# High parts of two weights fetched anew by GpSimd instead of kept, in a single-core decoder layer, with the planner's numbers and the order of stages set anew

## The chip, the cores and the metric

The kernel runs on one core of one Trainium2 chip. The metric is the device time of one execution in microseconds. Three runs of the kernel before took 2396.77, 2397.39 and 2397.78 us; the median, 2397.39, is what the changed kernel is compared with. A separate execution was profiled; its span, from the first to the last instruction, is 2396.1 us.

## What is computed

One layer on 2048 tokens of width 1024, in float32. The reference, cut to its core:

```python
h = rms_norm(x, mix_norm_g)
z = h @ w_in                                   # 1024 x 2048
lru_x, lru_gate, conf_a, conf_b = split(z, 4)  # 512 columns each
y_lru = rg_lru(causal_dwconv(lru_x), ...) * gelu(lru_gate)
c = silu(layer_norm(causal_dwconv(conf_a * sigmoid(conf_b))))   # 31 taps
x = x + concatenate([y_lru, c]) @ w_out        # 1024 x 1024
q = rms_norm(x) @ w_q;  k, v = split(rms_norm(mem) @ w_kv, 2)   # 256 memory tokens
x = x + softmax(q k / 16) v @ w_o              # 4 heads of 256
g, u = split(rms_norm(x) @ w_up, 2)            # 1024 x 6144
x = x + (gelu(causal_dwconv(g)) * u) @ w_down  # 3072 x 1024
return rms_norm(x)
```

## The kernel before, in words

**Products in three passes.** A float32 operand is split into a high half, rounded to the type float32r by a ScalarE (ACT) copy, and a low half, which VectorE (DVE) makes by subtracting the high half from the operand (`split`, line 578). `mm3` (line 586) then multiplies high by high, high by low and low by high. The tiles are called wh and wl for a weight, Xh/Xl, xh/xl, yh/yl and hidh/hidl for activations. Nearly all of TensorE's work is such triples of 128x512 matmuls.

**Tiles and quarters.** The sequence is cut into four quarters of 512 tokens. A *mixer* per quarter (`mixer`, with `conf` and `lru`) multiplies by `w_in`, in 8 groups of 256 columns, and runs the convolutions and the recurrence. For each group and each half kq of the rows, `project` (line 700) asks for two pairs (wh, wl) of 128 rows by 4 blocks by 128 columns, 256 KB a tile. Quarters 0 and 1 then go through attention one by one (`attend`, line 1254), and quarters 2 and 3 together (`attend_pair`, line 1760), in a form that needs fewer products and reads combined weights from `Folds`. Then come the up projection (`up` and `strassen_cols`) for each half of the sequence, and the down projection (`Down`). The memory's keys and values are folded into two matrices A and VO early on (`memory_a`, `memory_vo`), among the mixers.

**Where the weights come from.** A class for each of the two layouts hands them out:

- `Columns` (line 647) serves `w_in`. On the first call for a group it loads the raw columns (512 KB in pieces of 1 KB), splits them and, since they are wanted four times, writes all four tiles to a scratch area in DRAM (`Kept`, line 608) as rows of 2 KB. On later calls (n > 1) it reads both halves back from there.
- `Rows` (line 679) does the same for `w_out`, by 128 rows and 512 columns. With no raw weight (w is None) it hands out A and VO, which exist only in the scratch area.

All these transfers are issued by SyncE (SP), each after the semaphores that it needs: a store after its split, a load after the store of the same tile and after the last reader of the buffer that it goes into. GpSimd (POOL) issues only some small setup transfers at the start and computes nothing but the identity matrix.

**What sets the order.** Every operation and transfer is first recorded (`Program.do`, `Program.dma`, which is why the profile shows one line, L399, the emitter, for all of them). Generators for the stages are stepped by `drive`, in the order of the list TURNS and by a clock that counts TensorE work; each `yield n` gives way for n us of that clock. This fixes TensorE's order and which buffers follow each other. Then `deadlines` (line 239) gives every operation a due time, backwards from the products, and `schedule` (line 260) plays the program through: each engine takes the ready operation that is due first, 84 tiles of 2 KB a partition (slots "S") are handed out in order, and a transfer takes bytes / DMA_RATE on its issuer's own lane plus DMA_DELAY. Three passes are made, and the one that ends first is emitted. So DMA_DELAY, DMA_RATE and HOP_SAME (the assumed delay between two instructions of one engine) decide in which order each engine's queue is written, not what is in it.

**The constants around line 1976** are the waits and paces of the stages: for instance MEM_WAIT (when the memory's stage begins), MIX_WAIT and MIX_PACE (how the mixers are spread), EARLY (how many of the up projection's seven operand sets are made before it begins), FOLD_PACE and PAIR_WAIT (the pair's weights and its normalisations), NORMED (when each quarter's layer norm is done), and TURNS.

Of the kernel before, what the change touches and what calls it, by code (L numbers as in the profile page):

```python
# [17 lines left out]
P = 128  # L18
# [3 lines left out]
KQ = NK // 2  # L22
TT = 512
NQ = S // TT
# [24 lines left out]


HOP = 0.3
HOP_SAME = 0.1
DMA_DELAY = 2.5
DMA_RATE = 300e3
ACT_SWITCH = 1.3
ACT_PATIENCE = 8.0
POOL_LAST = 6.0
ISSUE = dict(SP=0.1, ACT=0.3, Pool=1.0)
# [74 lines left out]
class Program:  # L133
# [68 lines left out]
        o.calls.append((name, (out,) + args, kw))  # L202
        self.touch(o, [r.buf for r in ins] + list(reads), [r.buf for r in outs] + list(writes))

    def dma(self, out, in_, reads=(), writes=(), join=False, slack=30, by="SP"):


        o = self.op(by)
        o.moves = True
        refs = [r for r in (out, in_) if isinstance(r, Ref)]  # L210
        nbytes = max(int(np.prod(r.dummy.shape)) for r in refs) * 4
        o.cost, o.delay = nbytes / DMA_RATE, DMA_DELAY
        o.calls.append(("dma_start", (), dict(out=out, in_=in_)))
        rd = [in_.buf] if isinstance(in_, Ref) else []
        wr = [out.buf] if isinstance(out, Ref) else []
        o.store = slack if rd else False
        self.touch(o, rd + list(reads), wr + list(writes), join)
# [42 lines left out]
    def schedule(self):  # L260
# [3 lines left out]
        idle = {e: True for e in self.engines}  # L264
        free = {t: list(range(n)) for t, n in SLOTS.items()}
        queues = {t: list(reversed(q)) for t, q in self.queues.items()}
        table, dma_free, lag = [None], {e: 0.0 for e in ISSUE}, [0.0]
        order = []

        def push(t, kind, x):  # L270
            seq[0] += 1
            heapq.heappush(events, (t, seq[0], kind, x))
# [49 lines left out]
        def dispatch(e, t):  # L322
            if not idle[e]:
                return
            o = pick(e, t)
            if o is None:
                return
            idle[e] = False
            o.start, o.on = t, e
            order.append(o)  # L330
            if e == "PE":
                lag[0] += 0.2 * (t - o.turn - lag[0])
            cost = o.cost
            if e == "ACT" and o.sets is not None and table[0] not in o.sets:
                cost += ACT_SWITCH
                table[0] = o.sets[0]
            if o.either and e == "DVE":
                cost = estimate("DVE", "tensor_tensor", 1024, False)
            if o.moves:
                dma_free[e] = max(dma_free[e], t) + cost  # L340
                push(t + ISSUE[e], 2, e)
                push(dma_free[e] + o.delay, 0, o)
            else:
                push(t + cost, 2, e)
                push(t + cost, 0, o)
# [12 lines left out]
        while events:  # L358
            t, _, kind, o = heapq.heappop(events)
# [10 lines left out]
            else:  # L370
                for s in o.succs:
                    satisfied(s, t + (HOP_SAME if s.eng == o.on else HOP))
                for b in o.bufs:
# [49 lines left out]
def hybrid_layer(  # L423
# [17 lines left out]
    pr = Program(nc, place)  # L441
# [29 lines left out]
    def rnd(name, shape=None):  # L471
        return pr.new("S", shape, F32R, name)
# [7 lines left out]
    def spawn(gen, before=None):  # L480
        t = Task(gen)
        tasks.insert(tasks.index(before) if before else len(tasks), t)
        return t
# [160 lines left out]
    def flat(b):  # L644
        return Ref(b, (lambda ap: ap.rearrange("p k f -> p (k f)"),), np.broadcast_to(np.int8(0), (P, TT)))

    class Columns:
# [6 lines left out]
        def get(self, c0, kq):  # L654
            key = (c0, kq)
            n = self.seen[key] = self.seen.get(key, 0) + 1
            base = ((c0 // (2 * P)) * 2 + kq) * 4
            if n > 1:
                return [tuple(self.kept.get(base + 2 * f + i, (P, KQ, P), "w" + "hl"[i]) for i in range(2)) for f in range(2)]
            st = self.early.pop(key, None) or raw_cols(self.w, c0, kq)  # L660
            got = self.rounded(c0, kq, st)
            if n < self.uses:
                self.store(c0, kq, got)
            return got
# [5 lines left out]
        def rounded(self, c0, kq, st):  # L670
            return [split_cols(st, f) for f in range(2)]

        def store(self, c0, kq, got):
            base = ((c0 // (2 * P)) * 2 + kq) * 4
            for f in range(2):
                for i in range(2):
                    self.kept.put(base + 2 * f + i, flat(got[f][i]))

    class Rows:

# [4 lines left out]
        def get(self, k, half):  # L685
            base = (k * 2 + half) * 2
            n = self.seen[k, half] = self.seen.get((k, half), 0) + 1
            if n > 1 or self.w is None:
                return tuple(self.kept.get(base + i, None, "w" + "hl"[i]) for i in range(2))
            st = tmp("raw")  # L690
            pr.dma(st[:], self.w[k * P : (k + 1) * P, half * TT : (half + 1) * TT])
            hi, lo = pair("w")
            split(st[:], hi, lo)
            if n < self.uses:
                self.kept.put(base, hi[:])
                self.kept.put(base + 1, lo[:])
            return hi, lo

# [380 lines left out]
    attended = [Task(None) for _ in range(NQ)]  # L1079
# [893 lines left out]
        yield V_LATE  # L1973
        vec["v3072"] = columns([ffn_conv_w[0], ffn_conv_b], DFF, "v3072")

    EARLY, VO_WAIT, V_LATE, Z_COPIED = 5, 2, 500, (0, 1)
    MIX_WAIT, MIX_TURN, LN_SUM, LN_SQ, GATES = (5, 7, 6, 0), 5, 6, 0, 3
    MIX_PACE, ATT_PACE = (1, 4, 3, 4), ((0, 3, 0), (0, 2, 2), (6, 3, 3), (5, 9, 0))
    PAUSE, WARM = 2, 16
    FED = ("B21", "T2", "T1", "T3")  # L1980
    MEM_WAIT, VO_LATE, ATT_TURN, FFN_TURN, X_PACE, T_PACE = 17, 10, 1, (3, 8, 7, 24), 3, 10

    FOLDED = (2, 3)
    PAIR_WAIT, PAIR_TURN, FOLD_PACE = (0, 0, 9, 17), 7, (6, 7, 35)
    EARLY_AT, KEPT_AT = 6, 5
    FOLD_AT = lambda: ([turned_x[0]], [mem_a, turned_x[1]], [mem_vo])
    F_out, F_a, F_vo = Folds(W_out, "t_out"), Folds(A_rows, "t_a"), Folds(VO_rows, "t_vo")

    NORMED = [lambda: ([m[0]], 108), lambda: ([attended[0]], 31), lambda: ([m[2]], 26), lambda: ([m[3], n[2]], 6)]
    ATTEND = [lambda: [n[0]], lambda: [n[1]]]  # L1990
    TURNS = lambda: [later, first, fold, m[0], mem_a, m[1], first_t, a[0], n[2], m[3], n[0], n[3], mem_vo, n[1], m[2], a[1], a[2], tail]
    X = [HalfX(h) for h in range(NH)]

    def first_x():
# [6 lines left out]
    def feed_forward():  # L2001
        yield first
        yield attended[NQ - 1]
        spawn(X[1].kept(attends[NQ - 1], 20), tail)
        spawn(prepare_down(), tail)
        yield from up(0, X[0], X[1].make)
        down = Down()

        def ahead(key):
            if key in FED:  # L2010
                down.feed(0, FED.index(key))

        yield from up(1, X[1], ahead)
        yield from down.run()

    mixers, normeds, attends = ([Task(None) for _ in range(NQ)] for _ in range(3))
    later, mem_a, mem_vo, first_t, first, tail = (Task(None) for _ in range(6))
    m, n, a = mixers, normeds, attends
    for q in range(NQ):
        m[q].gen = mixer(q, m[q - 1] if q else None)  # L2020
        n[q].gen = normed(q, *NORMED[q]())
        if q not in FOLDED:
# [3 lines left out]
    fold = Task(fold_weights())  # L2026
# [36 lines left out]
```

## Time and profile before

| | |
|---|---|
| median of 3 runs | 2397.39 us (2396.77 to 2397.78) |
| span of the profiled execution, the only time given for it | 2396.1 us |
| TensorE (PE) busy | 2382.6 us, 99% |
| VectorE (DVE) busy | 2034.0 us, 85% |
| ScalarE (ACT) busy | 1313.2 us, 55% |
| GpSimd (POOL) busy | 11.2 us |
| HBM read, written | 409.36 MB, 192.94 MB |

How to read it: matmuls are pipelined, and the records give each a modelled end, so two that follow each other at full rate overlap and "busy" is the union of them. PEld is the loading of the weights into TensorE, which overlaps the products. A row of the waits gives the engine and what it writes, what ended the wait, the total in us, the number of waits and the longest. A row of a group gives its count, then busy time and mean ns of one, then the idle time of the engine just before it. A row of a transfer gives its issuer with a small q, the number of issues, the KB of each and the median us from issue to landing.

### The profile page before, as it was taken

The page shows a single profiled execution, that of the slowest core. Times are in us where ns is not written, and L with a number is a line of the kernel's source. Part 1 is how long each engine was busy: PE and PEld are TensorE (multiplying, and loading weights), DVE is VectorE, ACT ScalarE, POOL GpSimd, SP SyncE. Part 2 cuts the span into 40 slices and gives each one's busy share as a digit, 9 for nine tenths or more (in the row PEclk, how much of TensorE's full clock was granted, in tenths as well). Part 3 has the DMA queues.
Part 4 walks back from the last instruction along what each step waited for, and adds up shares of the span by engine and source line. Part 5 has one row for each costly group of instructions (what it writes and reads, how often), then busy time and mean ns, then how long its engine had stood idle before and what let it go on. Part 6 is the DMA issues. An engine that isn't in the chain of part 4 may idle for free.

```text
span 2396.1 us, 33483 instructions
## 1 busy us (share of the span) xinstructions
PE 2382.6 (99%) x10948; PEld 1974.5 (82%) x10948; DVE 2034.0 (85%) x3355; ACT 1313.2 (55%) x2374; POOL 11.2 (0%) x26
## 2 busy tenths in 40 slices
PE   9999999999999999999999999999999999999998
PEld 7898888888887888888888888888888888888887
DVE  7999994299899869879999887988988896676787
ACT  7772776357557678695555555554555541222333
POOL 1000000000000000000000000000000000000000
PEclk9999999999999999999999999999999999999999
DMA  9598789775878988787766544556565589887986
GB/s 351 197 296 309 234 300 305 254 255 176 296 261 271 318 277 280 268 289 265 252 234 208 194 172 158 175 177 211 190 216 199 186 303 324 283 280 254 312 303 258
DMA packets 363912, 604.56 MB, mean 252 GB/s; under 512 B 34809, under 2 KB 116985, under 8 KB 363738
## 3 DMA queue, kind: packets, MB, share of 16 engines
q1 hardware_dynamic: 362952, 601.81, 73.8%
q8 instruction: 86, 1.41, 0.2%
q14 instruction: 88, 0.72, 0.1%
q0 software_dynamic: 640, 0.36, 0.0%
q10 hardware_dynamic: 146, 0.27, 0.0%
HBM read 409.36 MB, written 192.94 MB: 251 GB/s over the span
## 4 chain that ended last, share of the span: by engine, by line
PE 94%; DVE 2%; ACT 2%; DMA 1%; issue 1%; SPq 0%; POOL 0%; DVEq 0%; POOLq 0%; ACTq 0%
PE ps L399 94%; DMA wl<-w_down 1%; DVE conv L399 1%; ACT L399 0%; DMA raw<-in_w_kv_dram 0%; ACT wh L399 0%; DVE wl L399 0%; ACT gate L399 0%; DVE x L399 0%; DVE s L399 0%; ACT yh L399 0%; DVE smalls L399 0%; DVE ptl L399 0%; ACT prob L399 0%; ACT conv L399 0%
## 5 line engine op out<-in xcount | busy, mean ns | idle before, releaser
L399 PE MATMUL ps<-Xh,wh 128*128 128x512 f32 x1344 | 523.3, 389 | 0.7 <-ACT u L399 0.7
L399 PE MATMUL ps<-Xh,wl 128*128 128x512 f32 x1344 | 523.2, 389 | 0.7 <-DVE wl L399 0.5
L399 PE MATMUL ps<-Xl,wh 128*128 128x512 f32 x1344 | 523.0, 389 | 0.0
L399 PE MATMUL ps<-wh,hidh 128*128 128x512 f32 x960 | 374.4, 390 | 0.0
L399 PE MATMUL ps<-wh,hidl 128*128 128x512 f32 x960 | 374.2, 390 | 0.1
L399 PE MATMUL ps<-wl,hidh 128*128 128x512 f32 x960 | 373.7, 389 | 0.0
L399 DVE SCALAR_TENSOR_TENSOR conv<-cb,v,conv 128x512 f32<-128x512 f32 x480 | 334.9, 741 | 1.8 <-ACT conv L399 0.9
L399 PEld LDWEIGHTS ps<-Xh,wl 128*128 128x128 f32 x1344 | 252.3, 188 | 54.0 <-DVE wl L399 1.5
L399 PEld LDWEIGHTS ps<-Xh,wh 128*128 128x128 f32 x1344 | 252.3, 188 | 53.1 <-ACT u L399 1.1
L399 PEld LDWEIGHTS ps<-Xl,wh 128*128 128x128 f32 x1344 | 252.3, 188 | 52.5
L399 ACT ACTIVATE hidh<-s 128x512 fp32r<-128x512 f32 x186 | 113.8, 631 | 271.6 <-DVE s L399 227.9
L399 PEld LDWEIGHTS ps<-wh,hidl 128*128 128x128 f32 x960 | 180.2, 188 | 39.5 <-DVE hidl L399 2.1
L399 PEld LDWEIGHTS ps<-wh,hidh 128*128 128x128 f32 x960 | 180.2, 188 | 37.8 <-ACT hidh L399 0.4
L399 PEld LDWEIGHTS ps<-wl,hidh 128*128 128x128 f32 x960 | 180.3, 188 | 37.2 <-DMA wl<-w_down 0.4
L399 PE MATMUL ps<-xh,wh 128*128 128x512 f32 x512 | 204.0, 398 | 0.1
L399 PE MATMUL ps<-xl,wh 128*128 128x512 f32 x512 | 199.6, 390 | 0.3 <-DVE xl L399 0.3
L399 PE MATMUL ps<-xh,wl 128*128 128x512 f32 x512 | 199.6, 390 | 0.0
L399 ACT ACTIVATE wh<-s 128x512 fp32r<-128x512 f32 x192 | 119.6, 629 | 117.6 <-DVE s L399 79.1
L399 ACT ACTIVATE wh<-raw 128x512 fp32r<-128x512 f32 (+2 forms) x214 | 127.4, 613 | 53.1 <-PE ps L399 21.6
L399 ACT ACTIVATE u<-ps 128x512 f32<-128x512 f32 x144 | 85.7, 595 | 126.0 <-PE ps L399 125.2
L399 DVE TENSOR_TENSOR acc<-acc,ps 128x512 f32<-128x512 f32 (+1 forms) x157 | 102.7, 678 | 59.5 <-PE ps L399 56.4
L399 DVE TENSOR_TENSOR wl<-raw,wh 128x512 fp32r<-128x512 f32 (+2 forms) x214 | 140.2, 668 | 12.0 <-ACT wh L399 10.7
(256 smaller groups left out, 4014.2 us busy)
## 6 DMA issues: line engine op xcount, KB each, us to landing
raw<-in_w_up_dram SPq DMA_DIRECT2D x96, 512.0 KB, 4.5
wh<-w_down SPq DMA_DIRECT2D x156, 256.0 KB, 4.9
wl<-w_down SPq DMA_DIRECT2D x156, 256.0 KB, 5.0
w_down<-wh SPq DMA_DIRECT2D x144, 256.0 KB, 3.1
w_down<-wl SPq DMA_DIRECT2D x144, 256.0 KB, 3.5
h<-hid SPq DMA_DIRECT2D x120, 256.0 KB, 4.7
wh<-w_in SPq DMA_DIRECT2D x96, 256.0 KB, 4.2
wl<-w_in SPq DMA_DIRECT2D x96, 256.0 KB, 4.7
```

The costliest lines, as they stand in the source:

```text
L399: getattr(e, name)(*[resolve(a) for a in args], **{k: resolve(a) for k, a in kw.items()})
```

## The change

Three things change.

1. `Columns.store` writes the low tiles alone, and `Rows.get` too. On later calls for `w_in` and `w_out` the high tile is made by a transfer from the raw float32 weight into a float32r tile, issued by GpSimd, and the low tile is read back as before. For `w_in` such a transfer reads 128 rows by 4 blocks in pieces of 512 bytes; for `w_out` 128 rows of 2 KB. A and VO stay as they were.
2. The planner's numbers: HOP_SAME, DMA_DELAY, DMA_RATE, and one lane that all issuers share instead of one for each.
3. The constants of the stages and the list TURNS.

```diff
-HOP_SAME = 0.1
-DMA_DELAY = 2.5
-DMA_RATE = 300e3
+HOP_SAME = 0.05
+DMA_DELAY = 5
+DMA_RATE = 350e3
...
-        table, dma_free, lag = [None], {e: 0.0 for e in ISSUE}, [0.0]
+        table, dma_free, lag = [None], [0.0], [0.0]
...
-                dma_free[e] = max(dma_free[e], t) + cost
+                dma_free[0] = max(dma_free[0], t) + cost
                 push(t + ISSUE[e], 2, e)
-                push(dma_free[e] + o.delay, 0, o)
+                push(dma_free[0] + o.delay, 0, o)
...
             if n > 1:
-                return [tuple(self.kept.get(base + 2 * f + i, (P, KQ, P), "w" + "hl"[i]) for i in range(2)) for f in range(2)]
+                return [self.again(c0 + f * P, kq, base + 2 * f + 1) for f in range(2)]
...
+        def again(self, c0, kq, low):
+            hi = rnd("wh", (P, KQ, P))
+            pr.dma(hi[:], self.w[kq * KQ * P : (kq + 1) * KQ * P, c0 : c0 + P].rearrange("(k p) f -> p k f", p=P), by="Pool")
+            return hi, self.kept.get(low, (P, KQ, P), "wl")
+
         def store(self, c0, kq, got):
             base = ((c0 // (2 * P)) * 2 + kq) * 4
             for f in range(2):
-                for i in range(2):
-                    self.kept.put(base + 2 * f + i, flat(got[f][i]))
+                self.kept.put(base + 2 * f + 1, flat(got[f][1]))
...
-            if n > 1 or self.w is None:
+            if n > 1 and self.w is not None:
+                hi = rnd("wh")
+                pr.dma(hi[:], self.w[k * P : (k + 1) * P, half * TT : (half + 1) * TT], by="Pool")
+                return hi, self.kept.get(base + 1, None, "wl")
+            if self.w is None:
                 return tuple(self.kept.get(base + i, None, "w" + "hl"[i]) for i in range(2))
...
             if n < self.uses:
-                self.kept.put(base, hi[:])
                 self.kept.put(base + 1, lo[:])
...
-    EARLY, VO_WAIT, V_LATE, Z_COPIED = 5, 2, 500, (0, 1)
-    MIX_WAIT, MIX_TURN, LN_SUM, LN_SQ, GATES = (5, 7, 6, 0), 5, 6, 0, 3
-    MIX_PACE, ATT_PACE = (1, 4, 3, 4), ((0, 3, 0), (0, 2, 2), (6, 3, 3), (5, 9, 0))
-    PAUSE, WARM = 2, 16
+    EARLY, VO_WAIT, V_LATE, Z_COPIED = 2, 3, 500, (0, 1)
+    MIX_WAIT, MIX_TURN, LN_SUM, LN_SQ, GATES = (5, 8, 10, 0), 4, 7, 0, 3
+    MIX_PACE, ATT_PACE = (0, 4, 3, 4), ((0, 3, 2), (0, 2, 0), (0, 0, 0), (0, 0, 0))
+    PAUSE, WARM = 1, 16
     FED = ("B21", "T2", "T1", "T3")
-    MEM_WAIT, VO_LATE, ATT_TURN, FFN_TURN, X_PACE, T_PACE = 17, 10, 1, (3, 8, 7, 24), 3, 10
+    MEM_WAIT, VO_LATE, ATT_TURN, FFN_TURN, X_PACE, T_PACE = 20, 11, 4, (5, 10, 0, 0), 0, 8
...
-    PAIR_WAIT, PAIR_TURN, FOLD_PACE = (0, 0, 9, 17), 7, (6, 7, 35)
+    PAIR_WAIT, PAIR_TURN, FOLD_PACE = (0, 0, 9, 28), 8, (3, 7, 33)
...
-    NORMED = [lambda: ([m[0]], 108), lambda: ([attended[0]], 31), lambda: ([m[2]], 26), lambda: ([m[3], n[2]], 6)]
+    NORMED = [lambda: ([m[0]], 108), lambda: ([attended[0]], 35), lambda: ([m[2]], 43), lambda: ([m[3], n[2]], 18)]
...
-    TURNS = lambda: [later, first, fold, m[0], mem_a, m[1], first_t, a[0], n[2], m[3], n[0], n[3], mem_vo, n[1], m[2], a[1], a[2], tail]
+    TURNS = lambda: [first, later, fold, m[0], mem_a, m[1], a[0], n[2], n[1], n[0], first_t, n[3], mem_vo, m[3], m[2], a[1], a[2], tail]
...
-        spawn(X[1].kept(attends[NQ - 1], 20), tail)
+        spawn(X[1].kept(attends[NQ - 1], 22), tail)
```

More of the change, by code (lines that the diff above doesn't have):

```diff
@@ L203, in do, with dma @@
         self.touch(o, [r.buf for r in ins] + list(reads), [r.buf for r in outs] + list(writes))
-    def dma(self, out, in_, reads=(), writes=(), join=False, slack=30, by="SP"):
+    def dma(self, out, in_, reads=(), writes=(), join=False, slack=30, by="SP", **more):
         o = self.op(by)
@@ L212, in dma @@
         o.cost, o.delay = nbytes / DMA_RATE, DMA_DELAY
-        o.calls.append(("dma_start", (), dict(out=out, in_=in_)))
+        o.calls.append(("dma_start", (), dict(out=out, in_=in_, **more)))
         rd = [in_.buf] if isinstance(in_, Ref) else []
```

## The prediction

> **What bounds the kernel now.** I read the page's head first, then PE's own waits, then a table of PE by stretches, because a kernel whose TensorE is nearly always busy can only win what TensorE still loses.
>
> ```profile
> span 2396.1 us, 33483 instructions
> PE 2382.6 (99%) x10948; PEld 1974.5 (82%) x10948; DVE 2034.0 (85%) x3355; ACT 1313.2 (55%) x2374; POOL 11.2 (0%) x26
> ```
>
> PE is idle for 2396.1 - 2382.6 = 13.5 us of the span. The median of the runs, 2397.39, is 1.3 us above this execution's span; I make the sum on the span and add 1.3. The waits of PE, longest first:
>
> ```profile
> PE ps L399 <- POOL ident masks.py:199: 2.4, 1, 2.4
> PE ps L399 <- DMA raw<-in_w_kv_dram: 1.5, 1, 1.5
> PE ps L399 <- ACT u L399: 0.7, 1, 0.7
> PE ps L399 <- DVE wl L399: 0.5, 1, 0.5
> PE ps L399 <- DVE x L399: 0.5, 1, 0.5
> ```
>
> One is the start, one is a late transfer, the rest are single waits on ACT or DVE. The table by stretches of 60 us shows where (columns: the stretch, its length, then each engine's busy time and count, PE, PEld, DVE, ACT, POOL; last the granted clock, DMA share and GB/s):
>
> ```profile
> 0.00:60.00 60.00, 57.31 (x288) 47.78 (x289) 47.13 (x111) 44.18 (x90) 11.18 (x26) 1.00 0.99 351
> ...
> 120.00:180.00 60.00, 58.50 (x395) 54.64 (x394) 59.80 (x98) 41.98 (x85) 0.00 (x0) 1.00 0.91 296
> ...
> 300.00:360.00 60.00, 59.31 (x280) 48.09 (x279) 58.68 (x93) 46.11 (x83) 0.00 (x0) 1.00 0.87 302
> ...
> 720.00:780.00 60.00, 59.48 (x281) 47.62 (x280) 59.56 (x96) 47.76 (x90) 0.00 (x0) 1.00 0.80 273
> ...
> 1380.00:1440.00 60.00, 60.00 (x267) 49.69 (x266) 51.30 (x83) 28.49 (x45) 0.00 (x0) 1.00 0.50 170
> 1440.00:1500.00 60.00, 59.31 (x261) 48.52 (x260) 44.66 (x71) 31.60 (x53) 0.00 (x0) 1.00 0.48 160
> 1500.00:1560.00 60.00, 59.31 (x262) 48.76 (x261) 57.63 (x92) 35.62 (x55) 0.00 (x0) 1.00 0.53 180
> ...
> 2220.00:2280.00 60.00, 60.00 (x263) 48.72 (x262) 41.59 (x74) 20.09 (x42) 0.00 (x0) 1.00 0.92 319
> 2280.00:2340.00 60.00, 59.95 (x263) 48.97 (x262) 47.30 (x84) 20.37 (x42) 0.00 (x0) 1.00 0.87 305
> 2340.00:2396.10 56.10, 49.45 (x217) 40.29 (x215) 44.23 (x89) 23.31 (x58) 0.00 (x0) 0.97 0.67 251
> ```
>
> Idle: 2.69 us in the first stretch, 6.65 in the last (the end, after the last product), and in the quoted middle 1.50 + 0.69 + 0.52 + 0.69 + 0.69 + 0.05 = 4.14. The granted clock is 1.00 in all but the last, so there is nothing to win in it. But the idle time is not all that is lost. Matmuls overlap in the records:
>
> ```profile
> 1700.20 0.39 PE L399 MATMUL ps<-Xh,wh 128*128 128x512 f32 x1
> 1700.43 0.39 PE L399 MATMUL ps<-Xl,wh 128*128 128x512 f32 x1
> ...
> 767.23 0.39 PE L399 MATMUL ps<-wh,ptl 128*128 128x512 f32 x1
> 767.73 1.13 PE L399 MATMUL ps<-sum,ones 128*128 128x512 f32 x2
> 768.29 0.80 PE L399 MATMUL ps<-wh,pth 128*128 128x512 f32 x1
> 768.92 0.39 PE L399 MATMUL ps<-wl,pth 128*128 128x512 f32 x1
> ```
>
> One starts every 0.23 us and is shown 0.39 us long, so a delay of up to 0.16 us shows as no idle at all. At 767.23 the next comes 0.50 us later (0.27 lost), at 768.29 it comes 0.63 later (0.40 lost). In the pure stretches counts do the same service: a full one has 267. The one at 1440 has six fewer (6 x 0.23 = 1.4, of which 0.69 was visible), at 1500 five fewer (1.15, 0.69 visible), at 2220 and 2280 four fewer (0.92 each, 0.05 visible in all). Hidden loss: 0.7 + 0.5 + 0.9 + 0.9 + 0.7 = 3.7. So what a better order could win is 4.1 + 3.7 = 7.8 us; the products are the same in number and size after the change, and start and end are not touched. The floor is 2397.4 - 7.8 = 2389.6, and it bounds every gain of this change.
>
> **The change part by part.** *Stores gone.* The high halves are no longer written.
>
> ```profile
> w_in<-wh SPq DMA_DIRECT2D x32, 256.0 KB, 5.9
> w_out<-wh SPq DMA_DIRECT2D x16, 256.0 KB, 3.5
> L399 SPq DMA_DIRECT2D wh<-w_in x96: 319/362/1107, 161.1 to 732.1; - x96
> L399 SPq DMA_DIRECT2D wh<-w_out x28: 319/367/442, 489.6 to 826.3; - x28
> SPq L399 <- PE ps L399: 437.6, 310, 14.4
> ```
>
> 48 stores of 262,144 bytes at 351 GB/s (the first stretch, DMA share 0.99) are 0.75 us each, 36 us of transfer time. The 32 of them for the input weights fall in the stretch where DMA is full. But PE's 2.69 us of idle there are the wait of 2.4 for its first operand and the start, so none of this is on the path: value 0 in PE time. SP also loses 48 + 96 + 28 = 172 issues of 0.36 us, 62 us; but that queue mostly waits for buffers that PE has to free (437.6 us in 310 waits), so this too I put at 0. No store must land before these 124 loads any more, which no wait of PE shows as a cost.
>
> *Loads moved to GpSimd.* 124 transfers go from SP's queue to a queue that only did setup, all of it in the first 60 us (26 instructions, 11.18 us). What they cost there:
>
> ```profile
> L399 POOL DMA_DIRECT2D tmp<-in_lru_w_a_dram x2 | 1.3, 660 | 0.0
> L399 POOL DMA_DIRECT2D raw<-in_lru_conv_b_dram x1 | 0.5, 515 | 0.0
> tmp<-in_lru_w_a_dram POOLq DMA_DIRECT2D x2, 64.0 KB, 5.4
> wh<-w_in SPq DMA_DIRECT2D x96, 256.0 KB, 4.2
> ```
>
> A GpSimd issue of one row is 515 ns, one of 256 pieces (64 rows by 4 blocks) is 660. The new one reads 128 x 4 pieces of 512 bytes: 515 + 512 x (145 / 255) = 0.81 us, an estimate from these rows, with 0.5 below it and 1.3 (twice 660) above. The tightest demand is a projection running alone: two such transfers for 24 products, 24 x 0.23 = 5.5 us, 2.7 us each. Even 1.3 is under half of that, so GpSimd does not become the bound. Behind a transfer that waits for its buffer stand only the other high parts; before, the low parts and all else on SP stood behind it too. Conversion while moving has no row. If it or the small pieces doubled the 0.75 us, 96 x 0.75 = 72 us of transfer time come in between 161 and 732 us, where the quoted stretches show shares of 0.80 to 0.91: 571 x 0.15 = 86 us are free. It fits, barely in the worst case.
>
> When do they land? A 64 KB transfer on GpSimd took 5.4 us to landing; 192 KB more at 351 GB/s give 5.9, with doubled transfer 6.7, and no less than the 4.2 of the same tile on SP. The new planner allows 0.75 + 5 = 5.75 us (it allowed 0.87 + 2.5 = 3.4). So a load that is issued at its due time lands 1 us late at worst, 1.5 early at best; I take 0.2 late, from the GpSimd row. [...]
>
> *Order set anew.* All loads are planned 2.4 us earlier, against landings of 4 to 6 us, so waits on transfers are where I expect the win: the 1.5 us for the key weights, and the losses of 0.9 + 0.9 in the down projection, where late weights lead the chain:
>
> ```profile
> 2311.85 6.47 DMA wl<-w_down
> ```
>
> That is 3.3. The other 7.8 - 3.3 = 4.5 hang on which ACT or DVE step runs first; between none and all, I take half, 2.2. Against this stand new stalls. EARLY goes from 5 to 2, so three of the operand sets for the up projection are rounded only when it begins:
>
> ```profile
> L399 DVE TENSOR_TENSOR Xl<-tx,Xh x32: 659/684/694, 1024.5 to 1501.9; 128x512 fp32r<-128x512 f32 x32
> ```
>
> 3 sets x 4 blocks x 0.684 = 8.2 us of DVE that used to lie ahead of it. One product of 12 matmuls lasts 2.7 us and so does a set, so they can just follow each other: between 0 and 8.2, I take 1, since the planner may still pull them forward. For landings on GpSimd that come late I take another 1, five of them at 0.2. Together 2.0 of new stalls.
>
> Sum: 2397.4 - 3.3 - 2.2 + 2.0 = 2393.9, forecast **2394.0**.
>
> **The rivals.** *A clean order.* The new numbers let nearly all of the 7.8 us go and GpSimd costs nothing: 2390. For it: six or seven stretches hold all of the loss, each with one cause. Against it: DVE is at 58 to 60 us of 60 in the quoted early stretches and any order leaves some chain late.
>
> *Late high parts.* The side that ends slower. Place: the first transfers of each column group of quarters 1 to 3, 24 groups, where a group's buffers come free late and its two high parts are issued just in time on one in-order queue. Price: if a transfer takes 6.7 us against the planned 5.75 and the second waits for the first's 0.81, a group starts 0.5 us late on average; 24 x 0.5 = 12 us, so 2394 + 12 = 2406. It decides once the landing exceeds 5.75 us by more than the lead that free buffers give. For it: the 5.4 us for 64 KB. Against it: PE had no wait on these loads when they were planned with 3.4 us and landed in 4.2.
>
> *Nothing moves.* Old stalls go and others of the same size come, as the products pace all: 2397.4.
>
> *GpSimd held up by DVE.* The rows for it are the long DVE chains in the stretches of the mixers:
>
> ```profile
> L399 DVE SCALAR_TENSOR_TENSOR conv<-cb,v,conv 128x512 f32<-128x512 f32 x384 | 267.5, 741 | 1.8 <-ACT conv L399 0.9
> ```
>
> If an issue could only proceed between four such instructions, it would last 0.81 + 4 x 0.74 = 3.8 us, above the 2.7 of a projection alone; a group's four transfers would fall 4.4 us behind, most of it covered by lead; with 1 us left in each of 24 groups, 2394 + 24 = 2418. [...] Against the rival: the 660 and 515 ns above were taken with DVE at work in the same stretch (47.13 of 60 us).
>
> **How the numbers follow.** A run of this kernel can tell about 0.2%, 4.8 us, from no change: faster is below 2392.6, slower above 2402.2. Chances: forecast 0.38 (some 0.05 of it below 2392.6), clean order 0.25, late high parts 0.20, nothing moves 0.13, DVE lock 0.04. That makes faster 0.30, same 0.47 (0.33 + 0.13 + a little of the late case), slower 0.23. The range starts at the floor, 2389.5, and reaches to 2406; outside are the worse half of the late case, the lock and a little below the floor.
>
> **What would show it.** Right: q0 carries some 32 MB, 124 transfers from GpSimd between 0.5 and 1.3 us of issue, 12.6 MB fewer written, no wait of PE on wh<-in_w_in, no wait on in_w_kv, 266 to 267 matmuls in every stretch of the down projection. Wrong: waits of PE on wh in the mixers, landings far over 6.7 us, GpSimd issues over 2.7 us, or a loss of several us at the start of the up projection with Xh or Xl as releaser. A PE busy time that differs by over 4 us in the sum of its products would refute the floor.

## The result, and the profile after

The changed kernel takes 2403.96 us (median of 10 runs, 2401.62 to 2405.53). The kernel before, run beside it, takes 2397.39 us (median of 10, 2396.57 to 2399.05). The ratio is 1.0027, with an interval from 1.0019 to 1.0035: slower by 6.6 us, a little more than the 0.2% set as the bound. The profiled execution of the changed kernel took 2403.8 us, and its span is 2401.9 us, 5.8 us longer than before.

The head of its page, the DMA queues and the transfers that were moved come first (of a transfer: its issuer, the count, the KB of each, the median us from issue to landing; of a queue: packets, MB, share of its time):

```profile
span 2401.9 us, 33543 instructions
PE 2385.6 (99%) x10948; PEld 1977.2 (82%) x10948; DVE 2034.3 (85%) x3355; ACT 1320.1 (55%) x2384; POOL 97.5 (4%) x150
...
q1 hardware_dynamic: 338184, 556.71, 67.6%
q0 software_dynamic: 55360, 32.88, 6.6%
...
HBM read 409.36 MB, written 180.36 MB: 246 GB/s over the span
...
wh<-in_w_in_dram POOLq DMA_DIRECT2D x96, 256.0 KB, 6.8
```

The 124 transfers are there: 32.88 MB on GpSimd's queue and 12.6 MB fewer written. TensorE has its 10948 products as before. VectorE's work is unchanged too, 2034 us, so nothing was added to either. ScalarE has 85 loads of an activation table instead of 75, 12.9 us more in all; they don't explain the loss, since e2 below has nearly the same loss with 76. The groups of GpSimd's issues (busy us, mean ns of one, then what they waited for):

```profile
L399 POOL DMA_DIRECT2D wh<-in_w_in_dram x96 | 71.4, 747 | 601.7 <-PE ps L399 217.5 <-DVE conv L399 169.7 <-DVE xl L399 89.5
L399 POOL DMA_DIRECT2D wh<-in_w_out_dram x28 | 15.1, 539 | 130.1 <-ACT hlast L399 44.4 <-PE ps L399 38.0 <-DMA t_out<-t_out 25.8
```

And TensorE's own waits, longest first:

```profile
PE ps L399 <- POOL ident masks.py:199: 2.4, 1, 2.4
PE ps L399 <- DVE ptl L399: 2.4, 1, 2.4
PE ps L399 <- DVE kvl L399: 1.9, 1, 1.9
PE ps L399 <- DVE xl L399: 1.3, 2, 1.0
PE ps L399 <- DVE vol L399: 0.5, 1, 0.5
PE ps L399 <- ACT hidh L399: 0.5, 1, 0.5
PE ps L399 <- DMA x<-in_x_dram: 0.4, 1, 0.4
```

No wait is for a wh that was fetched anew, and the 1.5 us for the key weights are gone. In their place stand waits for three low halves, which VectorE makes by one subtraction each. The stretches, to be held against those of before, show where (columns as there):

```profile
120.00:180.00 60.00, 58.98 (x394) 54.48 (x393) 58.21 (x97) 40.20 (x84) 6.34 (x9) 1.00 1.03 314
180.00:240.00 60.00, 58.13 (x251) 47.96 (x250) 55.96 (x85) 14.90 (x31) 10.76 (x15) 0.97 0.89 263
...
720.00:780.00 60.00, 57.61 (x266) 46.73 (x265) 59.62 (x98) 48.27 (x83) 3.51 (x6) 0.97 0.76 239
...
1020.00:1080.00 60.00, 60.00 (x283) 50.24 (x282) 46.28 (x78) 50.22 (x98) 0.00 (x0) 1.00 0.65 229
...
1440.00:1500.00 60.00, 60.00 (x267) 49.69 (x266) 50.51 (x83) 33.81 (x58) 0.00 (x0) 1.00 0.66 224
1500.00:1560.00 60.00, 60.00 (x267) 49.69 (x266) 56.78 (x91) 36.14 (x56) 0.00 (x0) 1.00 0.49 165
...
2220.00:2280.00 60.00, 59.29 (x260) 48.10 (x259) 44.79 (x79) 22.46 (x46) 0.00 (x0) 1.00 0.90 311
2280.00:2340.00 60.00, 60.00 (x264) 49.20 (x263) 48.40 (x85) 19.75 (x42) 0.00 (x0) 1.00 0.89 305
```

The two stretches from 1440 are full now, with 267 products each: that much was won. The two in the down projection (260 and 264) are no better than before. The new losses are at 180 and 720, and there the granted clock is 0.97 where it was 1.00; another 0.8 us is lost in the stretch from 240. A closer look at the first, in the timeline:

```profile
214.58 4.05 DVE L399 SCALAR_TENSOR_TENSOR conv<-cb,v,conv 128x512 f32<-128x512 f32 x6
...
215.60 0.63 ACT L399 ACTIVATE kvh<-ps 128x256 fp32r<-128x256 f32 x2
...
216.77 0.39 PE L399 MATMUL ps<-wl,kvh 128*128 128x512 f32 x1
...
218.56 0.41 DVE L399 TENSOR_TENSOR kvl<-ps,kvh 128x256 fp32r<-128x256 f32 x1
...
219.02 0.62 PE L399 MATMUL ps<-wh,kvl 128*128 128x512 f32 x1 [1.87 <-DVE kvl L399]
...
219.44 0.63 PE L399 MATMUL ps<-wh,kvh 128*128 128x512 f32 x1
...
219.87 0.63 PE L399 MATMUL ps<-wl,kvh 128*128 128x512 f32 x1
...
222.78 0.40 PE L399 MATMUL ps<-xh,wl 128*128 128x512 f32 x1
```

ScalarE has the high half ready at 216.2, but VectorE's queue holds further steps of the convolution, and the subtraction starts at 218.56. TensorE stands for 2 us. Then the products start 0.43 us apart where they start 0.23 apart elsewhere, until 222.7. The table by stretches gives that piece its clock:

```profile
219.30:222.70 3.40, 3.40 (x9) 2.61 (x9) 3.40 (x7) 1.27 (x3) 0.00 (x0) 0.50 1.01 249
222.70:226.00 3.30, 3.30 (x16) 2.68 (x16) 3.30 (x6) 0.16 (x2) 0.00 (x0) 1.00 0.05 9
```

At the granted clock of 0.50 some 8 products lose 0.2 us each, 1.5 us. The wait for ptl at 761 us has the same behind it. Together, from the starts of the products: two waits of 2.0 and 2.6 us and one of 1.2 at 172 us, and 2.9 us in the 16 products at half clock. From the first to the last product the kernel is 5.95 us longer. TensorE's busy time is 3.0 us of that, nearly all of it the half clock. The other 2.9 us are idle time between products, 7.45 us instead of 4.52, since old gaps went as the new ones came.

### The profile page after: what moved, and what is told of

Its sections match the earlier page's. It is cut to its first block, busy times and chain, and to the rows that moved or that the text cites. A ratio compares the mean times of both kernels' runs of the same rounds, so it can differ in the third digit from the quotient of the medians.

```text
span 2401.9 us, 33543 instructions
## 1 busy us (share of the span) xinstructions
PE 2385.6 (99%) x10948; PEld 1977.2 (82%) x10948; DVE 2034.3 (85%) x3355; ACT 1320.1 (55%) x2384; POOL 97.5 (4%) x150
## 3 DMA queue, kind: packets, MB, share of 16 engines
q1 hardware_dynamic: 338184, 556.71, 67.6%
q0 software_dynamic: 55360, 32.88, 6.6%
## 4 chain that ended last, share of the span: by engine, by line
PE 83%; DVE 2%; issue 2%; DMA 1%; ACT 1%; POOL 0%; SPq 0%; DVEq 0%; POOLq 0%; ACTq 0%
PE ps L399 83%; DVE conv L399 1%; DMA wh<-in_w_in_dram 1%; DVE wl L399 0%; ACT L399 0%; DMA wl<-VO 0%; DMA raw<-in_w_out_dram 0%; DVE xc L399 0%; ACT wh L399 0%; DVE x L399 0%; DVE t L399 0%; POOL wh L399 0%; DVE ptl L399 0%; DVE gate L399 0%; ACT gate L399 0%
```

## The experiments

The question is which part of the change costs the 6.6 us. My theory after the result: the transfers cost nearly nothing, and the order that the planner now writes is worse. The rival: the transfers (conversion, small pieces, a later landing) hold something up, and the order hides part of it. Each experiment has its own runs of the kernel before beside it, with medians of 2397.07 to 2397.78 us; ratios are against those.

**The parts alone (e1).** The kernel before with the new transfers; planner's numbers and stages as before, and the plan made anew.

```diff
-                return [tuple(self.kept.get(base + 2 * f + i, (P, KQ, P), "w" + "hl"[i]) for i in range(2)) for f in range(2)]
+                return [self.again(c0 + f * P, kq, base + 2 * f + 1) for f in range(2)]
...
+            if n > 1 and self.w is not None:
+                hi = rnd("wh")
+                pr.dma(hi[:], self.w[k * P : (k + 1) * P, half * TT : (half + 1) * TT], by="Pool")
```

> The kernel before with the fetching of the high parts alone: converting transfers from GpSimd, 48 stores fewer, planner's numbers and stages as before. Theory 'late parts' (the forecast's slower rival: transfers from GpSimd land later than planned and TensorE waits for wh): 2402 to 2409 us, with waits of PE on wh<-in_w_in in the mixers. Theory 'order' (the loss comes with the planner's numbers and the constants of the stages; the transfers are covered): 2395 to 2399 us, no wait of PE on wh. Theory 'chance' (any edit reshuffles which DVE step runs first, and a wait of PE of about 2 us here or there decides): anywhere in 2393 to 2406, with waits on small DVE steps such as kvl, ptl, xl.

Measured: 2420.10 us (2419.44 to 2423.34), ratio 1.0097 [1.0083, 1.0111]: 23 us slower, above all three ranges. TensorE's longest waits:

```profile
PE ps L399 <- ACT gate L399: 4.2, 1, 4.2
PE ps L399 <- DVE kvl L399: 2.9, 1, 2.9
PE ps L399 <- DVE ptl L399: 2.5, 1, 2.5
```

All on steps of ACT and DVE, none on wh. So either the plan alone does this, or the transfers disturb the engines without a wait that names them; e5 has the transfers without the new plan.

**The new order alone (e2).** The changed kernel with the high parts kept, as before; numbers and stages new, planned anew.

```diff
-                return [self.again(c0 + f * P, kq, base + 2 * f + 1) for f in range(2)]
+                return [tuple(self.kept.get(base + 2 * f + i, (P, KQ, P), "w" + "hl"[i]) for i in range(2)) for f in range(2)]
```

> The changed kernel with the high parts kept and read back by SyncE as before; planner's numbers and stages of the changed kernel. Theory 'late parts': 2394 to 2398 us, the new order without what hurts it. Theory 'order': 2402 to 2406 us, with waits on DVE steps near 217 and 761 us. Theory 'chance': anywhere in 2393 to 2406, and the waits are at other places than in the changed kernel.

Measured: 2402.84 us (2400.22 to 2404.58), ratio 1.0023 [1.0013, 1.0033]: 5.8 us slower with the old transfers. The waits for ptl (2.6 us at 762) and kvl (1.7 us at 216) are there without any converting transfer.

**The planner's numbers alone (e3), the stages alone (e4).** The kernel before, each with one half of the new order.

```diff
-HOP_SAME = 0.1
-DMA_DELAY = 2.5
-DMA_RATE = 300e3
+HOP_SAME = 0.05
+DMA_DELAY = 5
+DMA_RATE = 350e3
...
-        table, dma_free, lag = [None], {e: 0.0 for e in ISSUE}, [0.0]
+        table, dma_free, lag = [None], [0.0], [0.0]
```

```diff
-    EARLY, VO_WAIT, V_LATE, Z_COPIED = 5, 2, 500, (0, 1)
+    EARLY, VO_WAIT, V_LATE, Z_COPIED = 2, 3, 500, (0, 1)
...
-    TURNS = lambda: [later, first, fold, m[0], mem_a, m[1], first_t, a[0], n[2], m[3], n[0], n[3], mem_vo, n[1], m[2], a[1], a[2], tail]
+    TURNS = lambda: [first, later, fold, m[0], mem_a, m[1], a[0], n[2], n[1], n[0], first_t, n[3], mem_vo, m[3], m[2], a[1], a[2], tail]
```

> The kernel before with only the planner's numbers changed (HOP_SAME 0.05, DMA_DELAY 5, DMA_RATE 350e3, one shared lane). Prediction's step 'loads planned 2.4 us earlier win 3.3 us of waits on transfers': 2393 to 2395 us, no wait on in_w_kv. Theory 'order': if the numbers are what costs, 2400 to 2404 us. Theory 'chance': 2393 to 2403 with waits on DVE steps at new places.

> The kernel before with only the constants of the stages and the list of turns changed. Theory 'order': if the constants are what costs, 2400 to 2405 us. Theory 'late parts': 2395 to 2399 us. Theory 'chance': 2393 to 2406, waits on DVE steps at new places; constants that were set for other planner's numbers have no reason to fit here.

Measured: numbers 2403.68 us (2400.51 to 2404.30), ratio 1.0023 [1.0013, 1.0034]; stages 2402.89 us (2401.06 to 2406.39), ratio 1.0024 [1.0015, 1.0033]. Each costs some 6 us, and both together cost no more. Their losses are at different places: at the start, with a stretch at half clock, and in many small gaps in e3; at 394 us on xl, again with half clock, and at 764 on ptl in e4. Effects that don't add up and that move from place to place speak for a plan dealt anew each time more than for a bad constant.

**The transfers in the old order (e5, e6).** To part transfers from plan, the plan of before is made as it was, and only what is emitted changes: TensorE, VectorE and ScalarE keep their orders instruction by instruction. In e5 the 124 loads are converting transfers of GpSimd, at the place where SP had them, and the 48 stores are left out. In e6 the stores stay and GpSimd issues the plain loads of the kept high parts.

```diff
+            if raw is not None:
+                pr.ops[-1].via = "Pool"
+                pr.ops[-1].calls = [("dma_start", (), dict(out=b[:], in_=raw))]
...
-                    self.kept.put(base + 2 * f + i, flat(got[f][i]))
+                    self.kept.put(base + 2 * f + i, flat(got[f][i]), i == 0)
```

```diff
+            if raw is not None:
+                pr.ops[-1].via = "Pool"
```

> The kernel before with every instruction of PE, DVE and ACT in its old order; only the 124 loads of high parts are issued by GpSimd as converting transfers at the place where SyncE issued them, and the 48 stores are left out. Theory 'late parts' (the converting transfers themselves cost, by their length on the transfer engines and their landing): 2405 to 2420 us, that is most of the +23 us of the parts alone. Theory 'order' (the parts alone cost through the order that the planner made of them): 2396 to 2400 us.

> The same old order and all stores kept; the 124 loads of the kept high parts (rows of 2 KB, no conversion) are only issued by GpSimd instead of SyncE. Theory 'late parts by the queue' (GpSimd's issue and descriptors are what is slow): the same loss as with converting transfers. Theory 'late parts by the pieces' (pieces of 512 bytes double the transfer time, the queue is free): 2396 to 2399 us. Theory 'order': 2396 to 2399 us.

Measured: e5 2398.89 us (2396.77 to 2401.21), ratio 1.0004 [0.9995, 1.0014]; e6 2398.71 us (2396.94 to 2401.37), ratio 1.0006 [0.9997, 1.0015]. Neither can be told from the kernel before. The landings, e5 first, then e6:

```profile
wh<-in_w_in_dram POOLq DMA_DIRECT2D x96, 256.0 KB, 6.4
```

```profile
wh<-w_in POOLq DMA_DIRECT2D x96, 256.0 KB, 5.2
```

The move to GpSimd makes the landing 1.0 us longer than SP's 4.2, conversion and pieces another 1.2; TensorE notices neither. The rival falls for the old order: the same 124 transfers that stand beside a loss of 23 us in e1 cost 1.2 us here (-1.2 to +3.4 by the interval). What they cost within e1's own order isn't shown.

**The old transfers in the new order (e7).** The mirror of e5: the changed kernel's plan and its orders on TensorE, VectorE and ScalarE, with the high parts stored and read back by SP.

```diff
+            pr.ops[-1].via = "SP"
+            pr.ops[-1].calls = [("dma_start", (), dict(out=flat(hi).f32(), in_=self.kept.at(low - 1)))]
```

> The changed kernel with every instruction of PE, DVE and ACT in its new order; the high parts are stored and read back by SyncE again. Theory 'late parts': 2395 to 2399 us, the waits near 217 and 761 us go. Theory 'order' (the new order itself has the waits, whatever brings the weights): 2401 to 2405 us with the same two waits on kvl and ptl.

Measured: 2401.93 us (2401.14 to 2403.68), ratio 1.0017 [1.0008, 1.0026], 4.3 us slower than before. So most of the 6.6 us belongs to the order. The other 2 us, between this and the changed kernel, lie inside the overlap of the two intervals; whether the transfers cost that much in this order isn't settled. The wait for ptl is unchanged, that for kvl nearly gone (0.35 us by the starts), and others are new:

```profile
PE ps L401 <- DVE ptl L401: 2.4, 1, 2.4
PE ps L401 <- DVE x L401: 1.6, 1, 1.6
```

Where the wait for kvl begins can be read further up VectorE's queue. In the changed kernel VectorE works without a pause from 199.6 us to the late subtraction (18.86 of 18.96 us busy). Ahead of that it stood for 3.37 us, behind a ScalarE step that waited for a load of SP, the weight `w_o` before its split (raw). The changed kernel first, then e7, where the three engines have the same orders:

```profile
198.93 1.15 ACT L399 ACTIVATE wh<-raw 128x512 fp32r<-128x512 f32 x2 [7.56 <-DMA raw<-in_w_o_dram]
199.59 1.29 DVE L399 TENSOR_TENSOR wl<-raw,wh 128x512 fp32r<-128x512 f32 x2 [3.37 <-ACT wh L399]
```

```profile
198.83 1.29 DVE L401 TENSOR_TENSOR wl<-raw,wh 128x512 fp32r<-128x512 f32 x2 [1.77 <-ACT wh L401]
```

VectorE stands 1.6 us less in e7, and TensorE waits 1.7 us less for kvl. The kernel before has no such wait of VectorE between 145 and 220 us, and e2, with the old transfers, has one of 3.39. So the new order lets VectorE run dry behind a load some 18 us before TensorE feels it. The new transfers seem to add to it, though not as a wait on wh; how they do is not shown. Behind the wait for ptl there is no such stand: from 700 to 763 us VectorE is busy for 61.96 us of 63.

**How long a wait costs the clock (e8).** To measure the half clock by itself, 17 products of the up projection in the kernel before are held for lengths from 0.5 to 4.5 us, by ScalarE copies that the product must wait for and that change nothing in the result.

```diff
+HOLDS = ((), (128,), (512,), (512, 128), (512,) * 2, (512,) * 3, (512,) * 4, (512,) * 6)
...
+                if o.eng == "PE" and len(o.calls) == 3 * KH and o.calls[0][1][2].buf.name == "Xh":
+                    if nth % 20 == 10:
+                        self.hold(prev, o, HOLDS[nth // 20 % len(HOLDS)])
+                    nth += 1
```

> The kernel before with 17 holds added in the up projection, one at every 20th product: ACT reads the finished product, does 0 to 6 copies of 512 columns and rewrites the next weight's first column with its own value, so that TensorE waits; eight lengths, each twice, nothing else changed in what is computed. Theory 'clock' (a wait of TensorE of about 2 us or more halves its granted clock for 3.4 us, so it costs some 1.6 us more than its length): holds of up to about 1.6 us cost their length, those over 2 us show matmuls 0.43 us apart for about 3.4 us behind them; sum of the stalls some 35 us, half-speed extra another 10 to 15. Rival 'length alone' (the half-speed stretches seen in the changed kernel have another cause): all matmuls behind the holds stay 0.23 us apart.

Measured: one run, 2438.92 us, 41.2 us over the kernel before; the holds make some 32.5 us of that and the half clock 7.6. A hold's length is what the gap between two starts has over the usual 0.23 us. Stretches around a hold of 1.84 us, one of 2.50, one of 3.16 and another of 2.50 (the number ahead of the DMA share is the granted clock):

```profile
1294.00:1299.00 5.00, 3.33 (x16) 2.41 (x14) 3.19 (x6) 2.57 (x6) 0.00 (x0) 1.00 0.69 208
1351.00:1359.00 8.00, 5.66 (x19) 4.43 (x19) 3.97 (x8) 3.90 (x8) 0.00 (x0) 0.79 0.22 85
1409.00:1417.00 8.00, 5.00 (x16) 3.68 (x15) 1.33 (x3) 3.93 (x8) 0.00 (x0) 0.79 0.20 77
...
1810.00:1818.00 8.00, 5.66 (x25) 4.37 (x24) 3.67 (x6) 4.85 (x10) 0.00 (x0) 1.00 0.35 109
```

No hold up to 1.84 us (five lengths) brought the half clock. Of two holds of 2.50 us one did (1351) and one did not (1810): the same 5.66 us of busy TensorE hold 19 products in one and 25 in the other. The holds of 3.16 and 4.48 us did, each time. So five of the six holds of over 2 us had it. Each such stretch lasts 3.4 us and costs 1.4 to 1.6 us by the starts of the products.

Which holds have it follows from the clock records of the trace. The five stretches start at 1354.785, 1412.812, 1474.252, 1870.198 and 1931.637 us, which is 17, 18, 116 and 18 times 3.4133 us apart: in this run the clock changed on a grid of that step. The hold at 1351 has 2.03 of its 2.50 us within one step, and the next step runs at half clock. That at 1810 is cut by the grid into 1.70 and 0.80 us, and keeps the full clock. Over all holds, steps with up to 1.84 us of waiting were followed by full clock and steps with 2.47 us or more by half; of two steps with 2.02 and 2.03 us, only the one with 2.03 was. So what decided in this run was the idle time within one step, some 2 us, and not the length of the wait alone. In the changed kernel, too, some 2.0 us of idle time within one step sufficed (2.03 for kvl and 1.97 for ptl, by the starts).

**Is one more or less step of HOP as bad? (e9, e10, e15, e16).** If the order of before is a lucky one among many, then a change without any meaning should cost as much. HOP, the assumed delay from one engine to another, is moved by 0.01 us, in the kernel before (e9 up, e15 down) and in the changed one (e10 up, e16 down).

```diff
-HOP = 0.3
+HOP = 0.31
```

```diff
-HOP = 0.3
+HOP = 0.29
```

> The kernel before with one number of the planner moved by a hair, HOP 0.30 to 0.31 us. It means nothing for the chip; it only makes the planner write another order. Theory 'order by selection' (the kernel before is one good order among many of about 2403 us; any new plan with the same stages loses some 5 us): 2400 to 2406 us. Rival 'the changed numbers are worse in themselves' (the old numbers describe the chip better): 2396 to 2399 us, since 0.30 and 0.31 describe it equally.

> The changed kernel with HOP 0.30 to 0.31 us. Theory 'order by selection': 2400 to 2407 us, with the long waits at other places or of other sizes. Rival 'the changed numbers are worse in themselves': 2403 to 2405 us with the waits near 217 and 761 us as they were.

> The kernel before with HOP 0.30 to 0.29 us in the planner. Theory 'order by selection': 2400 to 2406 us again, as with 0.31. Rival (0.31 happened to be bad): 2396 to 2398 us.

> The changed kernel with HOP 0.30 to 0.29 us. Theory 'order by selection': 2400 to 2408 us; the changed kernel is an ordinary member of the spread, so this may fall on either side of its 2404.

Measured: e9 2401.67 us (2398.79 to 2403.35), ratio 1.0015 [1.0006, 1.0024]; e15 2399.70 us (2397.15 to 2401.22), ratio 1.0007 [0.9998, 1.0016]; e10 2405.42 us (2404.86 to 2405.43), ratio 1.0032 [1.0020, 1.0045]; e16 2403.29 us (2402.53 to 2405.16), ratio 1.0024 [1.0015, 1.0032]. A hundredth of a microsecond costs the old plan 4 us in one direction; in the other it costs 1.9 us, which lies between the two ranges expected and can't be told from nothing. It leaves the new plan where it was. The old plan stands at the lower end of its neighbours, and the new one is ordinary among its own. But three of each are few, and the three old ones (2397.4 to 2401.7 us) all lie below the three new ones (2403.3 to 2405.4). Nor have the new ones' losses moved far: the wait for kvl is near 217 us in e10 and e16 too, 1.6 us each. So the new numbers and stages may also be worse in themselves, and how the 6.6 us divide between that and the luck of the plan isn't settled.

**Is VectorE misjudged? (e11, e12).** The steps that came late are VectorE's. The part of a VectorE step that doesn't go by its size is 0.20 us in the planner for a step like the convolution's and 0.15 for others; the convolution's step takes 0.741 us and a subtraction 0.68, so here 0.28 and 0.22 are put in, in the old and in the new kernel.

```diff
-        return (0.2 if name == "scalar_tensor_tensor" else 0.15) + n * 0.0009
+        return (0.28 if name == "scalar_tensor_tensor" else 0.22) + n * 0.0009
```

> The kernel before; the planner's cost of DVE work set to what the profile shows: 0.741 us for a three-operand step on 512 columns (it assumed 0.66) and 0.68 for a two-operand one (it assumed 0.61). Theory 'DVE misjudged' (the long waits come because the planner thinks that DVE gets through its queue 10% sooner than it does): 2392 to 2397 us, no wait of PE on a DVE step over 0.6 us. Theory 'order by selection': 2399 to 2406 us, waits on DVE steps at new places.

> The changed kernel with the same corrected costs of DVE work. Theory 'DVE misjudged': 2395 to 2400 us, the waits on kvl near 217 and ptl near 761 us under 0.6 us. Theory 'order by selection': 2400 to 2407 us, with long waits on some other step.

Measured: e11 2414.66 us (2413.48 to 2417.80), ratio 1.0073 [1.0061, 1.0086]; e12 2420.23 us (2419.24 to 2420.89), ratio 1.0094 [1.0080, 1.0108], with a wait of 5.7 us on a sum. Both are above what either theory expected. Truer durations are no cure, so that theory falls; as other new plans lose too, it isn't shown that the durations themselves cost these 17 us.

**The late steps moved forward (e13, e14).** If the two waits are the loss, it should go when kvl and ptl, and the high halves kvh and pth on ScalarE, run as soon as their inputs are there. In the finished order these four are moved as far forward as their inputs and buffers allow; the queues of TensorE, SP and GpSimd stay as they are.

```diff
+FORWARD = ("kvh", "pth", "kvl", "ptl")
...
+        order = self.forward(list(order), slots)
```

> The changed kernel; in the finished order only the steps that split keys, values and probabilities (kvh and pth on ACT, kvl and ptl on DVE) are moved forward to where their inputs are made; PE, SyncE and GpSimd keep their queues. Theory 'two waits' (the loss is these two waits, 2.0 and 2.6 us, and 1.6 us of half speed behind each): 2396 to 2399 us, no half-speed stretch before the end. Rival 'spread' (DVE is behind by that much anyway, and the next step waits instead): 2401 to 2404 us, with waits of the same total on other steps of DVE.

> The kernel before with the same steps moved forward. Its waits on ptl near 757 and 768 us are only 0.3 and 0.4. Theory 'two waits': 2396 to 2398 us, nothing to win here. Rival 'spread': 2398 to 2403 us, since a step moved forward holds up DVE's chain.

Measured: e13 2418.00 us (2415.93 to 2418.92), ratio 1.0082 [1.0068, 1.0095], so 14 us slower than the changed kernel; e14 2407.75 us (2407.19 to 2408.00), ratio 1.0040 [1.0027, 1.0052]. Both are above every range expected. In e13, between 100 and 300 us, VectorE now waits itself, behind steps that it reaches before ScalarE has made their input:

```profile
DVE kvl L401 <- ACT kvh L401: 11.4, 8, 2.7
```

and TensorE pays elsewhere:

```profile
PE ps L401 <- DVE xl L401: 4.5, 5, 1.8
PE ps L401 <- DVE sum L401: 3.1, 1, 3.1
PE ps L401 <- DMA raw<-in_w_kv_dram: 2.8, 1, 2.8
```

So my picture of two late steps was too small. What it ran into shows in one row of each kernel, the 155 us from 145 on, where two mixers, the first attention and the folds lie together (busy TensorE, then loads, then VectorE). The kernel before, e5, the changed kernel, e13, in this order:

```profile
145.00:300.00 155.00, 154.46 (x763) 131.07 (x764) 153.38 (x242) 83.67 (x158) 0.00 (x0) 1.00 0.83 281
```

```profile
145.00:300.00 155.00, 153.90 (x759) 129.88 (x759) 152.85 (x242) 81.19 (x154) 23.21 (x32) 1.00 0.93 273
```

```profile
145.00:300.00 155.00, 151.31 (x737) 126.82 (x736) 149.02 (x235) 75.87 (x145) 21.05 (x29) 0.99 0.89 261
```

```profile
145.00:300.00 155.00, 148.92 (x729) 125.26 (x728) 145.73 (x229) 72.78 (x138) 20.79 (x28) 0.98 0.91 268
```

VectorE is idle for 1.6, 2.2, 6.0 and 9.3 us, TensorE for 0.5, 1.1, 3.7 and 6.1. In this stretch both engines are nearly full, and of these four the kernel before is the one in which they wait least. The stretch isn't the whole account: e4 has 153.79 us of TensorE and 153.69 of VectorE in it and is 5.8 us slower. That an idle VectorE is the cause is argued from the rows; what is shown is that with TensorE's queue held fixed, the order on VectorE and ScalarE alone moves the time by 10 us (e14) and 14 us (e13).

## Why the prediction was wrong, point by point

- **Stores gone, loads moved: right in the old order.** The price was put at 1 us of new stalls from late landings; e5 gives 1.2 (-1.2 to +3.4). In the new order, between e7 and the changed kernel, it may be 2. An issue of 512 pieces takes 747 ns against the estimate of 810, one of 128 rows 539.
- **Landing: the size was off.** 6.8 us against 5.9 taken and 6.7 as the bound. It cost TensorE no wait on wh, so the loads had lead enough; how much is not measured.
- **Transfer time: inside its bound.** By the queues' rows a MB takes 6.6% x 2401.9 / 32.88 = 4.8 us on q0 and 67.6% x 2401.9 / 556.71 = 2.9 on q1. That is 1.65 times as much, where twice was allowed for.
- **EARLY: 1 us was set against it, and nothing shows.** The stretch from 1020 has TensorE at 60.00 of 60, and no wait of TensorE on Xh or Xl is in the list.
- **The step that failed is "Order set anew".** It said 3.3 us won from transfers planned earlier, and of the other 4.5 "between none and all, I take half, 2.2". Of the named wins, the 1.5 for the key weights came and the 0.9 + 0.9 in the down projection did not; the losses at 1440 and 1500 went as well. But the plan brought new waits on other engines' steps, of 2.0, 2.6 and 1.2 us, and two stretches at half clock behind them, 2.9 us. With the old transfers the order costs 4.3 us in e7 and 5.8 in e2, where the sum had it win 5.5, or 4.5 after the 1 us for EARLY. One fault is in "between none and all": none, a win of zero, was no lower bound, since a plan dealt anew can lose as well as win. The other is that planning loads earlier was to end waits on transfers: in the changed kernel ScalarE waits 7.6 us at once for the raw `w_o`, and VectorE 3.4 behind it.
- **The loss in the down projection was misread.** "Late weights lead the chain" was taken from one transfer. The waits of the weight loads in the kernel before, from 2220 to 2340 us, are mostly for VectorE:

```profile
PEld ps L399 <- DVE hidl L399: 1.1, 3, 0.4
PEld ps L399 <- ACT hidh L399: 0.4, 1, 0.4
PEld ps L399 <- DMA wl<-w_down: 0.4, 1, 0.4
```

  So some 0.4 of the 1.8 us hung on a transfer, and loads planned earlier had no hold on the rest.
- **What I didn't ask of the profile:** how good the order of before already was. It lost 7.8 us in 2397. With VectorE busy for 153.4 of 155 us in the tightest stretch, I take that to be close to what an order can reach there. Nine kernels above were planned anew with the planner's VectorE costs as they were (the changed kernel, e1 to e4, e9, e10, e15, e16): eight lie 4 to 23 us above it, and e15 can't be told from it.
- **The half clock was not in the sum.** The granted clock was read as "nothing to win", and not as something to lose. A wait of over 2 us was priced at its own length; five of the six in e8 cost 1.4 to 1.6 us more.
- **The rivals.** *A clean order*, 2390, did not come. Of *late high parts* the time, 2406, came close and the mechanism did not: no wait on wh. *Nothing moves* had the mechanism, old stalls that go and others that come, but took them as equal. *GpSimd held up by DVE* did not happen: none of its 124 issues took over 0.79 us, in stretches with VectorE at up to 59.9 of 60 us. That an issue could only proceed between four of VectorE's steps was the author's assumption, and no run shows it.
- **The floor** stands: no kernel came below it, and TensorE's busy sum rose by 3.0 us, of which the half clock is 2.9.

What stays open: why the new plan puts the step on the raw `w_o` ahead of its landing and places ptl so late, how far its model is off in 145 to 300 us, and how much of the loss is the plan's luck. Truer VectorE costs and earlier steps both made it worse, and no order better than that of before was found. e5 can't be told from it in time and writes 12.6 MB less.

## What to carry to other kernels

When a planner writes the queues, an edit of one transfer deals every queue anew. Test the edit first with the finished order held fixed, as in e5, and only then let the planner run; otherwise its luck is taken for the edit's price (1.2 us against 23 here). Before counting idle time as something to win, see whether the second busiest engine is full in the same stretch: if so, the order of before may be the best within reach, and a new one is as likely to lose. A wait of two microseconds or more on TensorE is to be priced with the half clock behind it: five of the six in e8 had it, at 1.4 to 1.6 us. And a late step is to be followed back along its engine's queue: the wait for kvl began 18 us earlier, behind a load.

## What the runs showed of the hardware

- In these traces TensorE's granted clock fell to 0.50 on a grid of 3.413 us steps (five stretches in e8; the two of the changed kernel start 160 steps apart), when some 2 us of the step before were idle. In e8, among products that follow each other without a gap, 1.84 us never sufficed. The wait of 2.6 us for ptl had it in the changed kernel's profile, with 1.97 us of it in one step, and not in that of e7, with 1.81. In e9 two waits in one step did it together, of 1.4 and 1.0 us before 758 us, among products of 128 columns. Most stretches lasted one step, 3.4 us; e1 has two of 6.8 us, e13 one, and e12 one of 10.2.
- This is part of why the changed kernel's runs spread over 3.9 us where those of before spread over 2.5: the run with a mean granted clock of 1.000 took 2401.62 us, the three with 0.999 took 2402.43 to 2404.12, the six with 0.998 took 2403.09 to 2405.53.
- A converting transfer of 128 x 4 pieces of 512 bytes landed in 6.4 us (e1, e5) and 6.8 us (the changed kernel, single ones in 3.2 to 12.2) by the medians, a plain one of 2 KB rows from the same queue in 5.2 (e6), and from SP in 4.2 (the kernel before).
